# Sparse attention of one block in a single written order: products between the groups of heads, the index sum on TensorE

## The chip, the cores and the metric

The kernel runs on one core of a Trainium2 chip. A core has five engines that run side by side, each with its own list of instructions: TensorE (PE, matrix products), VectorE (DVE), ScalarE (ACT), GpSimd (POOL) and SyncE (SP, which here only starts transfers). They wait for one another by semaphores. The metric is the device time of one execution in microseconds (us). The profile adds the clock that TensorE was granted, as a share of its full 2.4 GHz; the lower of its two levels, 1.2 GHz, reads 0.50.

## The reference

The model is two blocks on 256 tokens of width 1024, with a batch of one. Only one part of the first block is touched by the change, the sparse attention (16 heads of 64 for the queries; one key and one value head; 8 index heads):

```python
def sparse_attention(h, cos, sin, w_in, q_norm, k_norm, w_out, topk):
    q, k, v, qi, ki, wi = split_cols(h @ w_in, SA_SPLITS)
    q = apply_rope(rms_norm(q...), cos, sin); k = ...; qi, ki = apply_rope(...)
    # for each block of 128 queries:
    logits = einsum('bthd,bsd->btsh', qi, ki)
    score = einsum('btsh,bth->bts', relu(logits), wi) * idx_scale
    score = where(causal, score, -inf)
    _, sel = top_k(score, topk)                  # 64 keys of each row
    s = einsum('bthd,btkd->bthk', q, k[sel]) * att_scale
    p = softmax(where(valid, s, -inf))
    o = einsum('bthk,btkd->bthd', p, v[sel])
    return o @ w_out
```

The kernel does not gather. It finds the 64 largest scores of a row, and adds 0 to the logits of the chosen keys and a very negative number to all others.

## The kernel before, in words

**Products.** Every weight matrix is kept in float32 and split into two float32r parts, hi (a copy by ACT, line 201) and lo (the difference, line 205, in pieces of 512 columns; where `help` is set, POOL takes the second piece). A product is then three matmuls, hi by hi, hi by lo and lo by hi (`mm3`, lines 276, 277 and 278), most of them 512 columns wide. `fetch` loads 128x2048 of weights (three such buffers), `halve` makes hi and lo of one half (four of each).

**Sparse attention.** Tokens come as two tiles t of 128. The steps have a letter each. P: the products of key, value, index key and index weights (200 columns). K: their rope (norm and rotation). J: the transposes to kT. R and T: rope and transposes of the index queries of a tile. L: the index logits, a matmul of 64 partitions for each of 8 heads, and relu into `rl`. S: the index sum (lines 978 to 991): on DVE, eight operations a tile that add relu times the weight of the head to a running sum, then the causal limit. C: the choice of the 64 largest, two rounds of 8 in each of four parts (lines 1002 and 1003), and the bias. U and M: load of and product with the query weights of a group g of 8 heads. Q and X: scale and rope of a group and tile. Y: its transposes.

**Attention proper** goes through 12 items (t, g, b): the scores of four heads (tile 0, 128 keys) or two heads (tile 1, 256 keys), 512 columns each. A (`attend`, line 1059): matmuls into one PSUM bank, then on DVE the sum with the bias and the maximum of every head (1062, 1064). Z (`exps`, 1072): exponentials on ACT. B (`probs`, 1081, 1083): four transposes on PE and a copy by ACT. O (`values`, 1092): products with the values. F (`finish`): division by the sums, and four transposes (`flip`, line 433) with a split, which make the stationary operand of the output product. In the loop, round i issues A of item i, Z of item i-1, B of i-2 and O of i-3.

**What sets the order.** Inside this part every engine takes its instructions in the order in which the program writes them. `ORDER` gives all steps up to the first item, then, between bars, what goes in after the A of each round. W loads a unit of the output weights, and D is one step of `down_steps`, the output product (8 k-tiles, two halves of 512 columns, two token tiles). The last two D begin after the last bar of items; the final part of `down_steps` issues the last k-tiles together with the entry of the next part. `mid` there does the transposes of the fourth finished group (line 433, at 923.42 us in the profiled execution); from that point on both kernels do the same work.

Of the kernel before, what the change touches and what calls it, by code (L numbers as in the profile page):

```python
# [18 lines left out]
T = 256  # L19
# [9 lines left out]
class Wide:  # L29
    """Transposed activations, split in two float32r parts: k-tiles of [128 features, 256 tokens]."""  # L30
# [72 lines left out]
class Net:  # L103
# [52 lines left out]
    def consts(self):  # L156
# [40 lines left out]

# [9 lines left out]
    def rsqrt(self, v, n, scale=1.0, add=EPS):  # L207
        """1 / sqrt(v * scale + add), [128, n]; add may be a column."""
# [9 lines left out]
    def row_rstd(self, x):  # L218
        """[128, 1] of 1/sqrt(mean(x*x) + eps), x [128, 1024]."""
# [6 lines left out]
    def softplus(self, y, n):  # L226
        """max(y, 0) + log1p(exp(-|y|)); log1p(u) = 2 atanh(u / (2 + u)) as a series (|argument| <= 1/3)."""
# [31 lines left out]
    def halve(self, raw, h, help=False):  # L259
        """Half h of the columns as (hi, lo)."""  # L260
# [7 lines left out]
    def unit(self, dram, cols=2048, help=(0, 0)):  # L268
        """Load [128, cols], give two (hi, lo) halves."""
# [3 lines left out]
    def mm3(self, out, a, b, start, stop):  # L273
        """out += a^T b with a = (hi, lo), b = (hi, lo)."""
# [15 lines left out]
    def group_steps(self, dram, hT):  # L290
        """group_x in two steps, a yield in between."""
# [14 lines left out]
    def weave(self, main, side, done):  # L306
        """Emit main, with as many steps of side as it gives in between; done gets an item when main is through."""
# [25 lines left out]
    def down_steps(self, dram, n, aT, done, then, ready={}, mid=lambda: None):  # L333
# [4 lines left out]
        acc = [[self.ps() for _ in range(2)] for _ in range(2)]  # L338
        def go(t, cb, kk, w):
            s = slice(cb * 512, cb * 512 + 512)  # L340
            self.mm3(acc[t][cb], aT(kk, t), (w[0][:, s], w[1][:, s]), kk == 0, kk == n - 1)
        late = []
        for u in range(n // 2):
            for h, w in enumerate(ready.get(u) or self.unit(dram[u])):
# [7 lines left out]
            yield  # L352
        a, b, *cd = late
# [4 lines left out]
        def last(t, cb):  # L358
            for k in cd:
                go(t, cb, *k)  # L360
            done(t, cb, acc[t][cb])
# [8 lines left out]
        with self.manual():  # L370
            whole(0, a)
            whole(0, b)
            mid()
# [50 lines left out]
    def to_T(self, t, src, aT, gain=None):  # L424
        """src [128 tokens, 1024] -> k-tiles of aT for token tile t (times gain[:, k])."""
# [3 lines left out]
    def flip(self, src, aT, b, t, gain=None):  # L429
        """src [128 tokens, 512] -> half b of aT, token tile t."""  # L430
# [5 lines left out]
    def put_T(self, p, aT, b, t, gain):  # L436
        """Transposed [128, 4, 128] in PSUM (times gain) -> half b of aT, token tile t."""
# [4 lines left out]
        # the two engines take turns at a PSUM bank: each all of it at a time  # L442
# [37 lines left out]
    def start(self, dram):  # L480
        """The first part's start: loads in the order of their use; the clock of TensorE is up by then."""
# [57 lines left out]
class Hybrid:  # L539
    def hybrid(self, then):  # L540
# [8 lines left out]
        def products():  # L549
            """The wide products that only wait for the input: z, q, k, v and the output gate."""  # L550
# [30 lines left out]
        def chain():  # L581
            """Gives how many steps of the wide products may go in here."""
# [38 lines left out]
            bc = self.g().rearrange("p (j t c) -> p j t c", j=4, t=2)     # B0 B1 C0 C1  # L621
# [10 lines left out]
            def inputs(g):  # L632
                """x of one group of 8 heads, token-major, before its activation"""
# [9 lines left out]
            def states(g):  # L643
# [4 lines left out]
                # state after the first chunk: B^T (x dt decay)  # L648
# [7 lines left out]
            def decays(g):  # L656
                """per chunk of 128 tokens: scores times decays [s, head, t]"""
# [44 lines left out]
            # scores C B^T (transposed), B of the first chunk token-major  # L702
# [32 lines left out]
            R = self.t2()                   # R0 R1 wi wk rows  # L735
# [13 lines left out]
            w = self.small(16)              # exp(-m_t) (2 chunks), w_inter, state weights  # L749
# [25 lines left out]
            # state of the first chunk  # L775
# [67 lines left out]
ORDER = ("P0 P1 R0 U00 K U01 R1 M000 T0 J M001 L0 T1 S0 U10 C00 M010 M011 L1 X00 C01 S1 M100 C02 X01 Q00 C03 M101 "  # L843
         "Y00 C10 U11 C11 Q01 Y01 C12 | C13 M110 | M111 X10 |  | Y10 X11 |  | Q10 Q11 Y11 |  |  |  |  |  | "
         "W0 | D | W1 | D | ")
SHARE = ((0, 0), (0, 0), (1, 1), (1, 1), (1, 1), (1, 1))

TURN = (0, 0, 0, 1, 0, 1)


class Sparse:
    def rope_setup(self):
        """cos and sin of position * frequency, [128, 2, 32] each."""
# [14 lines left out]
        self.cs = self.const(128)           # cos (2 x 32), sin (2 x 32)  # L868
# [4 lines left out]
        # tables (c, s) times the gain of q; times that of k, and plain for the index key  # L873
# [15 lines left out]
    def rope(self, out, x, c, s, H, copies=1, help=0):  # L889
        """out[:, h, copy, :] = x rotated; c, s [128, H or 1, 2, 32] broadcast; x [128, H, 64]."""  # L890
        V = self.nc.vector
        W = self.nc.gpsimd if help else V
# [9 lines left out]
        W.tensor_tensor(o5[:, :, :, 0], both(a4[:, :, 0]), both(b4[:, :, 1]), OP.subtract)  # L902
        W.tensor_tensor(o5[:, :, :, 1], both(a4[:, :, 1]), both(b4[:, :, 0]), OP.add)

    def sparse(self, then):
# [6 lines left out]
        plain = lambda f, t: cs[:, f, t][:, None, None].to_broadcast([128, 8, 2, 32])  # L912
        gained = lambda f, t: self.cq4(f)[:, t].rearrange("p (h d) -> p h d", h=2)[:, None].to_broadcast([128, 8, 2, 32])

# [5 lines left out]
        kk = self.t2().rearrange("p (h r d) -> p h r d", h=4, r=2)    # (t, i), twice  # L920

        def keys(u):
            for h, w in enumerate(self.unit(ins["saw"][:, u * 800:(u + 1) * 800], 800)):
                hi, lo = (a.rearrange("p (k c) -> p k c", k=2) for a in w)
                for k in range(2):
                    i = 4 * u + 2 * h + k
                    for t in range(2):
                        self.mm3(pk[t][:, :200], hT.tok(i, t), (hi[:, k, :], lo[:, k, :]), i == 0, i == 7)

        def key_rope():  # L930
            ss = self.small(2)
            for t in range(2):
                A.activation(kv[:, t, :200], pk[t][:, :200], AF.Copy)
                A.activation(self.junk[:, :64], pk[t][:, :64], AF.Square, accum_out=ss[:, t:t + 1])
            r = self.rsqrt(ss, 2, 1.0 / 64)
            c, s = (self.ck[:, f * 256:f * 256 + 256].rearrange("p (h f d) -> p h f d", h=4, f=2) for f in range(2))
            self.rope(kk, kv.rearrange("p t (i d) -> p (t i) d", i=2)[:, :, :64], c, s, 4, 2)
# [847 lines left out]
```

## Time and profile before

| | |
|---|---|
| time, median of 3 runs | 1735.54 us (1732.81 to 1738.21) |
| the profiled execution: its span | 1757.1 us, 23,334 instructions |
| TensorE busy | 1720.3 us, 98% of the span |
| VectorE, ScalarE, GpSimd busy | 63%, 51%, 18% |
| loaded from memory | 283 MB, 163 GB/s over the span |
| the touched part | about 811 to 923 us of the span |

The profiled execution took its span of 1757.1 us with the profiler on, 1.2% more than the median of the runs; times inside it are read against its own span. A "busy" PE is a PE with a matmul in flight, at whichever clock: the share of 98% does not tell how fast it went. Durations of matmuls overlap, so that the cost of one in a sequence is the distance from start to start.

### The profile page before, as it was taken

What the parts mean: (1) busy time and instruction counts of PE and PEld (TensorE: products, weight loads), DVE (VectorE), ACT (ScalarE), POOL (GpSimd) and SP (SyncE); (2) the same over time, 40 slices, a digit from 0 to 9 for tenths busy, and PEclk for the clock granted to TensorE, in tenths of its full rate; (3) what the DMA queues carried; (4) which work ended last, traced back from release to release, by engine and by line L of the source; (5) the groups of instructions that cost most, each with busy time, mean ns of one, the idle gap of its engine ahead of it and who ended that gap; (6) DMA issues with size and microseconds to landing.
All of it is one profiled execution on the core that took longest, in us unless ns stands there. A gap on an engine that the chain in (4) does not pass through costs nothing.

```text
span 1757.1 us, 23334 instructions
## 1 busy us (share of the span) xinstructions
PE 1720.3 (98%) x8742; PEld 1437.8 (82%) x8742; DVE 1111.6 (63%) x2107; ACT 902.7 (51%) x1323; POOL 318.1 (18%) x466
## 2 busy tenths in 40 slices
PE   9999999999999999999899999999999999999998
PEld 7888799887888888887688888788898878879886
DVE  6555588666555565547736564557775765678565
ACT  6544476465444454435445544466446446745643
POOL 3000121001000100002311000233632124264211
PEclk9999999999999999999669999999999999999999
DMA  7545453445455554554114555455544444544442
GB/s 269 189 173 199 146 192 121 144 158 185 173 191 191 180 184 176 193 188 151 40 66 174 192 174 216 140 174 168 156 145 150 158 155 168 168 134 167 156 144 96
DMA packets 63425, 287.40 MB, mean 164 GB/s; under 512 B 23760, under 2 KB 26704, under 8 KB 30288
## 3 DMA queue, kind: packets, MB, share of 16 engines
q1 hardware_dynamic: 63312, 285.92, 46.5%
q8 instruction: 68, 1.11, 0.3%
q14 instruction: 45, 0.37, 0.1%
HBM read 283.28 MB, written 2.62 MB: 163 GB/s over the span
## 4 chain that ended last, share of the span: by engine, by line
PE 81%; POOL 6%; DVE 4%; issue 4%; DMA 2%; ACT 2%; SPq 1%; POOLq 0%; ACTq 0%; DVEq 0%
PE mm L277 24%; PE mm L278 24%; PE mm L276 24%; POOL g L1320 2%; POOL g L1318 2%; PE tr L433 1%; PE tr L468 1%; DMA g<-dram 1%; ACT hi L201 1%; DVE lo L205 1%; POOL lo L205 1%; DMA dram<-g 1%; DVE g L85 1%; POOL sm L215 0%; DVE g L987 0%
## 5 line engine op out<-in xcount | busy, mean ns | idle before, releaser
L205 DVE TENSOR_TENSOR lo<-raw,hi 128x512 fp32r<-128x512 f32 (+1 forms) x1024 | 694.8, 720 | 406.1 <-ACT hi L201 404.6
L201 ACT ACTIVATE hi<-raw 128x1024 fp32r<-128x1024 f32 x530 | 551.5, 1045 | 455.3 <-PE mm L278 317.7
L277 PE MATMUL mm<-lo,g 128*128 128x512 f32 (+1 forms) x1440 | 576.9, 401 | 0.8 <-DVE lo L205 0.5
L276 PE MATMUL mm<-hi,g 128*128 128x512 f32 (+1 forms) x1440 | 576.5, 403 | 0.7 <-ACT g L201 0.7
L278 PE MATMUL mm<-hi,g 128*128 128x512 f32 (+1 forms) x1440 | 571.5, 397 | 0.3 <-DVE g L446 0.2
L278 PEld LDWEIGHTS mm<-hi,g 128*128 128x128 f32 x1440 | 273.8, 190 | 62.8 <-DVE g L205 1.6
L277 PEld LDWEIGHTS mm<-lo,g 128*128 128x128 f32 x1440 | 274.0, 190 | 61.5 <-DVE lo L205 3.9
L276 PEld LDWEIGHTS mm<-hi,g 128*128 128x128 f32 x1440 | 273.9, 190 | 60.2 <-ACT g L201 1.2
L277 PE MATMUL mm<-lo,f 128*128 128x512 f32 x416 | 165.2, 397 | 0.2 <-POOL lo L205 0.2
L278 PE MATMUL mm<-hi,f 128*128 128x512 f32 x416 | 164.8, 397 | 0.0
L276 PE MATMUL mm<-hi,f 128*128 128x512 f32 x416 | 163.6, 400 | 0.0
L276 PE MATMUL mm<-g,hi 128*128 128x256 f32 x480 | 136.3, 284 | 0.0
L278 PE MATMUL mm<-g,lo 128*128 128x256 f32 x480 | 135.8, 285 | 0.0
L277 PE MATMUL mm<-g,hi 128*128 128x256 f32 x480 | 135.2, 282 | 0.0
L212 POOL TENSOR_SCALAR sm<-sm 128x1 f32<-128x1 f32 x18 | 9.4, 521 | 562.2 <-ACT c L70 561.1
L277 PEld LDWEIGHTS mm<-lo,f 128*128 128x128 f32 x416 | 78.4, 188 | 19.0 <-POOL lo L205 0.6
L278 PEld LDWEIGHTS mm<-hi,f 128*128 128x128 f32 x416 | 78.3, 188 | 18.5
L276 PEld LDWEIGHTS mm<-hi,f 128*128 128x128 f32 x416 | 78.5, 189 | 18.2
L276 PEld LDWEIGHTS mm<-g,hi 128*128 128x128 f32 x480 | 90.6, 189 | 0.7 <-issue 0.2
L277 PEld LDWEIGHTS mm<-g,hi 128*128 128x128 f32 x480 | 90.5, 189 | 0.3
L278 PEld LDWEIGHTS mm<-g,lo 128*128 128x128 f32 x480 | 90.1, 188 | 0.4 <-issue 0.2
L201 ACT ACTIVATE g<-tr 128x512 fp32r<-128x512 f32 x48 | 28.1, 595 | 86.9 <-PE tr L433 57.1
(387 smaller groups left out, 1693.9 us busy)
## 6 DMA issues: line engine op xcount, KB each, us to landing
raw<-in_wgu_dram SPq DMA_DIRECT2D x86, 1024.0 KB, 4.8
raw<-in_wdn_dram SPq DMA_DIRECT2D x44, 1024.0 KB, 4.8
raw<-in_bx_dram SPq DMA_DIRECT2D x24, 1024.0 KB, 4.9
raw<-in_bgate_dram SPq DMA_DIRECT2D x24, 1024.0 KB, 4.9
raw<-in_bw_dram SPq DMA_DIRECT2D x20, 1024.0 KB, 5.0
raw<-in_hyx_dram SPq DMA_DIRECT2D x12, 1024.0 KB, 4.8
raw<-in_bproj_dram SPq DMA_DIRECT2D x12, 1024.0 KB, 5.0
raw<-in_hyw_dram SPq DMA_DIRECT2D x10, 1024.0 KB, 4.8
```

The costliest lines, as they stand in the source:

```text
L85: self.nc.vector.scalar_tensor_tensor(self.src[t][:, s], self.net.x[t][:, s], self.rstd[t], self.gain[:, s], op0=OP.mult, op1=OP.mult)
L201: nc.scalar.activation(hi, src, AF.Copy)
L205: (nc.gpsimd if o and help else nc.vector).tensor_tensor(lo[..., s], src[..., s], hi[..., s].bitcast(F32), OP.subtract)
L212: G.tensor_scalar(r, v, add, EPS, op0=OP.add, op1=OP.add)
L276: mm(out, a[0], b[0], start=start, stop=False)
L277: mm(out, a[0], b[1], start=False, stop=False)
L278: mm(out, a[1], b[0], start=False, stop=stop)
L433: self.nc.tensor.transpose(p[:, k, :], src[:, k * 128:(k + 1) * 128], self.ident)
L468: nc.tensor.transpose(p[:, t, j, :], hd[:, j * 128:(j + 1) * 128], self.ident)
L1318: G.tensor_tensor(a, Z[:, :m, e:e + 1].to_broadcast([128, m, n]), B[:, e:e + 1, cs].to_broadcast([128, m, n]), OP.mult)
L1320: G.tensor_tensor(Z[:, :m, cs], Z[:, :m, cs], a, OP.add)
```

## The change

The part gets one written order for all its steps, the rounds of items included, and smaller steps: query loads by half a unit (U), query products by k-tile (M for both token tiles of group 0, N for one of group 1), output loads by half (W), and output products by token tile, k-tile and column half (D). A product of one k-tile and one token tile is three matmuls; group 1 has sixteen. In before, eight of these precede the first item and eight follow the A of items 0 and 1, and all output products but those left to a later step follow the A of the last item. Now fourteen of the sixteen and 20 output products stand between the steps of the items. The keys are loaded in one fetch of 1600 columns with two halves of 800 in place of four of 400; the rope of the key is done apart from that of the index key. No piece of lo and no rope is on POOL any more.

The index sum becomes matmuls: ACT scales the identity by the weight of each head (`index_weights`, 16 copies of 128x128), and eight float32 matmuls a tile add diagonal times relu in a PSUM bank (`index_scores`). ACT copies the first half of tile 1; DVE keeps the causal limit.

```diff
-ORDER = ("P0 P1 R0 U00 K U01 R1 M000 T0 J M001 L0 T1 S0 U10 C00 M010 M011 L1 X00 C01 S1 M100 C02 X01 Q00 C03 M101 "
-         "Y00 C10 U11 C11 Q01 Y01 C12 | C13 M110 | M111 X10 |  | Y10 X11 |  | Q10 Q11 Y11 |  |  |  |  |  | "
-         "W0 | D | W1 | D | ")
-SHARE = ((0, 0), (0, 0), (1, 1), (1, 1), (1, 1), (1, 1))
-TURN = (0, 0, 0, 1, 0, 1)
+ORDER = (
+    "H0 R0 H1 P0 P1 U000 R1 U001 E U010 T0 M00 K1 G0 J1 U011 T1 L0 M01 S0 K0 M02 L1 U100 G1 C00 J0 M03 C01 S1 U101 "
+    "M04 C02 M05 U110 C03 M06 C10 M07 Q00 U111 X00 Q01 C11 N00 X01 N01 Y00 C12 "
+    "A0 N02 Z0 N03 Y01 C13 N04 "
+    "A1 N05 B0 Z1 N06 N07 O0 Q10 "
+    "A2 N10 B1 Z2 N11 N12 O1 X10 F0 "
...
+    "A7 D021 B6 Z7 I1 D031 O6 "
...
+    "A11 D041 W30 B10 Z11 D050 O10 "
+    "W31 B11 D051 O11 F3")
...
+        def index_weights(t):
+            dg[t] = self.g(1024).rearrange("p (h s) -> p h s", h=8)
+            for h in range(8):
+                A.activation(dg[t][:, h, :], self.ident, AF.Copy, scale=wi[:, t, h:h + 1])
...
         def index_scores(t):
             S = 128 * (t + 1)
-            z = sc[t] = self.g(256)
+            z = sc[t] = self.l2(256)
+            pz = self.pt()[:, :S]
             for jb in range(2):
                 for r in range(2):
                     for i in range(2):
-                        h = 4 * jb + 2 * i + r
-                        x = rl[t, jb, r][:, i, :S]
-                        if jb + r + i:
-                            V.scalar_tensor_tensor(z[:, :S], x, wi[:, t, h:h + 1], z[:, :S], op0=OP.mult, op1=OP.add)
-                        else:
-                            V.tensor_scalar(z[:, :S], x, wi[:, t, h:h + 1], None, op0=OP.mult)
-            tr = z[:, S - 128:S]
-            V.tensor_tensor(tr, tr, self.causal, OP.min)
+                        mm(pz, dg[t][:, 4 * jb + 2 * i + r, :], rl[t, jb, r][:, i, :S], start=jb + r + i == 0,
+                           stop=jb + r + i == 3)
+            if t:
+                A.activation(z[:, :128], pz[:, :128], AF.Copy)
+            V.tensor_tensor(z[:, S - 128:S], pz[:, S - 128:], self.causal, OP.min)
...
-            w[g, u] = self.unit(ins["sax"][2 + 2 * g + u], help=SHARE[2 * g + u])
+            if h == 0:
+                w[g, u] = self.fetch(ins["sax"][2 + 2 * g + u])
+            w[g, u, h] = self.halve(w[g, u], h)
...
+        def down(t, kk, cb):
+            go(t, cb, kk, w["o", kk])
...
-            first, *then_ = ORDER.split("|")
-            do(first)
-            late = []
-            for i, names in enumerate(then_):
...
+            for o in ORDER.split():
+                args = (int(o[1:]),) if o[0] in "AZBO" else map(int, o[1:])
+                steps[o[0]](*args)
+        self.down_end(go, acc, [(k, w["o", k]) for k in range(4, 8)], self.add_x, then, lambda: turned(3))
```

On PE, in the middle of the items, before (1059 is A, 1081 B, 1092 O, 433 the transposes of a finished group):

```order
L1092 MATMUL tr_7299<-l_985_6824,t_1131_7426 128x64 x4
L1059 MATMUL mm_7460<-l_987_6826,g_7333 128x128 x4
L1081 MATMUL tr_7475<-c_71,t_1118_7379 128x128 x4
L1092 MATMUL tr_7299<-l_985_6824,t_1139_7454 128x64 x4
L1059 MATMUL mm_7490<-l_987_6826,g_7410 128x256 x2
L1081 MATMUL tr_7501<-c_71,t_1137_7437 128x128 x4
```

And after, on PE between the A of items 6 and 7 (1100 is A, 1123 B, 1135 O, 1078 Y; 276 to 278 are an output product):

```order
L1100 MATMUL mm_7502<-l_987_6826,g_7430 128x128 x4
L276 MATMUL mm_7463<-hi_7467,f_6829 128x512
L277 MATMUL mm_7463<-lo_7468,f_6829 128x512
L278 MATMUL mm_7463<-hi_7467,f_6830 128x512
L1123 MATMUL tr_7516<-c_71,t_1135_7457 128x128 x4
L1078 MATMUL tr_7527<-c_71,t_1140_7481 128x128 x4
L276 MATMUL mm_7534<-hi_7370,f_6829 128x512
L277 MATMUL mm_7534<-lo_7371,f_6829 128x512
L278 MATMUL mm_7534<-hi_7370,f_6830 128x512
...
L1135 MATMUL tr_7314<-l_985_6824,t_1150_7521 128x64 x4
L1100 MATMUL mm_7548<-l_987_6826,g_7430 128x128 x4
```

The narrow matmuls of an item are the same; three output products of three matmuls each have come between two A (one is left out here).

On DVE, the index sum of tile 1, before (989, 987 and 991 are the sum, 1002 and 1003 the choice for tile 0):

```order
L1003 MATCH_REPLACE l_1034_7044<-sm_7105,l_1034_7044 128x128
L989 TENSOR_SCALAR g_7108<-t_1038_7078,sm_6825 128x256
L987 SCALAR_TENSOR_TENSOR g_7108<-t_1038_7078,sm_6825,g_7108 128x256
L987 SCALAR_TENSOR_TENSOR g_7108<-t_1040_7083,sm_6825,g_7108 128x256 x2
L987 SCALAR_TENSOR_TENSOR g_7108<-t_1042_7088,sm_6825,g_7108 128x256 x2
L987 SCALAR_TENSOR_TENSOR g_7108<-t_1044_7093,sm_6825,g_7108 128x256 x2
L991 TENSOR_TENSOR g_7108<-g_7108,c_82 128x128
L1002 MAX sm_7132<-l_1034_7044 128x8
```

And after, on DVE from the end of the first half of U01 to the first choice of tile 0 (1028 is the causal limit of tile 0, which now reads a PSUM bank; 921 to 974 are the rope of the key):

```order
L205 TENSOR_TENSOR lo_6967<-raw_6925,hi_6966 128x512 x2
L1028 TENSOR_TENSOR l_1027_7004<-tr_7005,c_82 128x128
L921 TENSOR_TENSOR t_1030_7020<-l_985_6824,c_286 128x128
L922 TENSOR_TENSOR t_1031_7021<-l_985_6824,c_286 128x128
L923 TENSOR_TENSOR t_988_6827<-t_1030_7020,t_1031_7021 128x2x2x32
L924 TENSOR_TENSOR t_988_6827<-t_1030_7020,t_1031_7021 128x2x2x32
L974 TENSOR_TENSOR t_988_6827<-t_988_6827,sm_7017 128x2x128
L205 TENSOR_TENSOR lo_7056<-raw_7053,hi_7055 128x512 x2
L1039 MAX sm_7070<-l_1027_7004 128x8
```

Of the sum only the limit is left on DVE; the splits and the rope of the key stand behind it.

## Rows read from the trace of the kernel before

**Rows 1.** The page: the span, and the granted clock in 40 slices.
```profile
span 1757.1 us, 23334 instructions
...
PEclk9999999999999999999669999999999999999999
```

**Rows 2.** Windows: us, busy (count) of PE, PEld, DVE, ACT, POOL, PEclk, DMA, GB/s.
```profile
811.00:838.00 27.00, 27.00 (x166) 22.64 (x165) 24.34 (x57) 12.92 (x25) 3.57 (x4) 1.00 0.54 194
838.00:845.00 7.00, 1.82 (x10) 1.18 (x8) 6.55 (x22) 3.08 (x4) 2.43 (x4) 0.72 0.00 0
845.00:862.00 17.00, 14.73 (x59) 10.91 (x60) 16.24 (x57) 6.71 (x20) 6.50 (x9) 0.80 0.26 93
862.00:904.40 42.40, 42.40 (x163) 36.01 (x162) 16.50 (x68) 22.41 (x63) 8.49 (x12) 0.50 0.00 1
904.40:923.40 19.00, 18.81 (x94) 15.26 (x94) 8.74 (x12) 8.26 (x13) 3.49 (x2) 0.96 0.45 166
```

**Rows 3.** Groups on DVE, 811 to 862 us: count, busy us, mean ns, idle before.
```profile
L205 DVE TENSOR_TENSOR lo<-raw,hi 128x512 fp32r<-128x512 f32 x12 | 9.5, 849 | 0.0
L987 DVE SCALAR_TENSOR_TENSOR g<-t,sm,g 128x128 f32<-128x128 f32 x7 | 4.3, 620 | 0.5
...
L987 DVE SCALAR_TENSOR_TENSOR g<-t,sm,g 128x256 f32<-128x256 f32 x7 | 3.4, 485 | 0.5
...
L902 DVE TENSOR_TENSOR t<-t,t 128x256 f32<-128x256 f32 x5 | 2.1, 424 | 0.2
```

**Rows 4.** Timeline of DVE: start us, us, line, operation.
```profile
846.57 3.26 DVE L205 TENSOR_TENSOR lo<-raw,hi 128x512 fp32r<-128x512 f32 x2
...
854.02 0.28 DVE L1062 CUSTOM_DVE_ANT_0 t<-mm,l 128x128 f32<-128x128 f32 x1
```

**Rows 5.** ACT: the relus of tile 1; durations of scaled copies 128x128 (min/median/max).
```profile
831.50 2.07 ACT L976 ACTIVATE t<-tr 128x512 f32<-128x512 f32 x4 [4.12 <-PE tr L973]
...
L444 ACT ACTIVATE g<-tr,c x32: 349/368/408, 4.8 to 1669.0; 128x128 fp32r<-128x128 f32 x32
```

**Rows 6.** Timeline of PE, index logits of tile 1 to the first items.
```profile
830.33 2.10 PE L973 MATMUL tr<-l,g 64*128 64x256 f32 x16
...
843.85 1.11 PE L1039 MATMUL tr<-c,t 128*128 128x128 f32 x4 [5.18 <-POOL t L903]
...
853.45 0.50 PE L276 MATMUL mm<-hi,g 128*128 128x512 f32 x1
853.78 0.39 PE L277 MATMUL mm<-lo,g 128*128 128x512 f32 x1
...
856.42 1.13 PE L1059 MATMUL mm<-l,g 64*128 64x256 f32 x4
857.48 0.66 PE L1081 MATMUL tr<-c,t 128*128 128x128 f32 x4
```

**Rows 7.** Timeline of PE among the items: A of two rounds.
```profile
864.01 2.07 PE L1059 MATMUL mm<-l,g 64*128 64x256 f32 x4
...
868.66 2.07 PE L1059 MATMUL mm<-l,g 64*128 64x256 f32 x4
```

**Rows 8.** Timeline of PE, output products and the last steps of items.
```profile
906.13 0.40 PE L277 MATMUL mm<-lo,f 128*128 128x512 f32 x1
...
910.80 0.60 PE L1081 MATMUL tr<-c,t 128*128 128x128 f32 x4
911.23 1.00 PE L1092 MATMUL tr<-l,t 128*128 128x64 f32 x8
912.07 0.61 PE L1081 MATMUL tr<-c,t 128*128 128x128 f32 x4
...
923.42 0.60 PE L433 MATMUL tr<-c,t 128*128 128x128 f32 x4
```

**Rows 9.** Windows again: the clock's rise after the items; a stretch of another part.
```profile
904.40:905.90 1.50, 1.50 (x6) 1.21 (x6) 0.00 (x0) 1.26 (x5) 0.00 (x0) 0.50 0.97 235
...
1672.40:1679.20 6.80, 6.80 (x48) 6.25 (x47) 2.62 (x7) 2.94 (x3) 0.00 (x0) 1.00 0.11 48
```

More of the change, by code (lines that the diff above doesn't have):

```diff
@@ L331, in down, with down_go, down_steps @@
             pass
-    def down_steps(self, dram, n, aT, done, then, ready={}, mid=lambda: None):
-        acc = [[self.ps() for _ in range(2)] for _ in range(2)]
+    def down_go(self, n, aT):
+        acc = {}
         def go(t, cb, kk, w):
             s = slice(cb * 512, cb * 512 + 512)
-            self.mm3(acc[t][cb], aT(kk, t), (w[0][:, s], w[1][:, s]), kk == 0, kk == n - 1)
+            if (t, cb) not in acc:
+                acc[t, cb] = self.ps()
+            self.mm3(acc[t, cb], aT(kk, t), (w[0][:, s], w[1][:, s]), kk == 0, kk == n - 1)
+        return go, acc
+    def down_steps(self, dram, n, aT, done, then):
+        go, acc = self.down_go(n, aT)
         late = []
         for u in range(n // 2):
-            for h, w in enumerate(ready.get(u) or self.unit(dram[u])):
+            for h, w in enumerate(self.unit(dram[u])):
                 kk = 2 * u + h
@@ L352, in down_steps, with down_end @@
             yield
+        self.down_end(go, acc, late, done, then)
+    def down_end(self, go, acc, late, done, then, mid=None):
         a, b, *cd = late
@@ L370, in down_steps @@
         with self.manual():
-            whole(0, a)
-            whole(0, b)
-            mid()
+            if mid:
+                mid()
+            else:
+                whole(0, a)
+                whole(0, b)
             if E.norm:
@@ L887, in ck5, with rope @@
         return self.ck[:, f * 256:f * 256 + 256].rearrange("p (t i d) -> p t i d", t=2, i=2)[:, :, i]
-    def rope(self, out, x, c, s, H, copies=1, help=0):
+    def rope(self, out, x, c, s, H, copies=1):
         V = self.nc.vector
-        W = self.nc.gpsimd if help else V
         n = H * 64
@@ L901, in rope @@
         V.tensor_tensor(b4, x4, s, OP.mult)
[L902 to L903 removed]
+        V.tensor_tensor(o5[:, :, :, 0], both(a4[:, :, 0]), both(b4[:, :, 1]), OP.subtract)
+        V.tensor_tensor(o5[:, :, :, 1], both(a4[:, :, 1]), both(b4[:, :, 0]), OP.add)
     def sparse(self, then):
@@ L919, in sparse @@
         v = kv[:, :, 64:128]
-        kk = self.t2().rearrange("p (h r d) -> p h r d", h=4, r=2)
-        def keys(u):
[L923 to L928, printed above, removed]
@@ L930, in key_rope @@
-        def key_rope():
-            ss = self.small(2)
-            for t in range(2):
[L933 to L937, printed above, removed]
-            k = kk.rearrange("p (t i) r d -> p t i (r d)", t=2)[:, :, 0]
-            V.tensor_tensor(k, k, r[:, :, None].to_broadcast([128, 2, 128]), OP.mult)
-            V.tensor_scalar(wi, kv[:, :, 192:200], 8.0 ** -0.5 * 64.0 ** -0.5, None, op0=OP.mult)
@@ L942, in key_flip, with key_load @@
-        def key_flip():
-            pT = self.pt().rearrange("p (i t s) -> p i t s", i=2, t=2)
-            for t in range(2):
-                for i in range(2):
-                    PE.transpose(pT[:, i, t], kk[:, 2 * t + i].rearrange("p r d -> p (r d)"), self.ident)
-            A.activation(kT, pT, AF.Copy)
+        kk = self.t2().rearrange("p (t i r d) -> p t i r d", t=2, i=2, r=2)
+        key_ss = self.small(2)
+        w = {}
+        def key_load(u):
+            if u == 0:
+                w["k"] = self.fetch(ins["saw"], 1600)
+            w["k", u] = self.halve(w["k"], u)
@@ new lines, in keys, with key_out @@
+        def keys(u):
+            hi, lo = (a.rearrange("p (k c) -> p k c", k=4) for a in w["k", u])
+            for k in range(4):
+                i = 4 * u + k
+                for t in range(2):
+                    self.mm3(pk[t][:, :200], hT.tok(i, t), (hi[:, k, :], lo[:, k, :]), i == 0, i == 7)
+        def key_out():
+            for t in range(2):
+                A.activation(kv[:, t, :192], pk[t][:, :192], AF.Copy)
+            for t in range(2):
+                A.activation(wi[:, t], pk[t][:, 192:200], AF.Copy, scale=8.0 ** -0.5 * 64.0 ** -0.5)
@@ new lines, in key_rope @@
+        def key_rope(i):
+            if i == 0:
+                for t in range(2):
+                    A.activation(self.junk[:, :64], kv[:, t, :64], AF.Square, accum_out=key_ss[:, t:t + 1])
+                r = self.rsqrt(key_ss, 2, 1.0 / 64)
+            c, s = (self.ck5(f, i) for f in range(2))
+            k = kk[:, :, i]
+            self.rope(k, kv[:, :, 128 * i:128 * i + 64], c4(c), c4(s), 2, 2)
+            if i == 0:
+                k = k.rearrange("p t r d -> p t (r d)")
+                V.tensor_tensor(k, k, r[:, :, None].to_broadcast([128, 2, 128]), OP.mult)
@@ L950, in sparse, with key_flip @@
+        def key_flip(i):
+            pT = self.pt()[:, :256].rearrange("p (t s) -> p t s", t=2)
+            for t in range(2):
+                PE.transpose(pT[:, t], kk[:, t, i].rearrange("p r d -> p (r d)"), self.ident)
+            A.activation(kT[:, i], pT, AF.Copy)
         pq = {}
-        half = lambda S: kT[:, 1].rearrange("p t s -> p (t s)")[:, :S]
         v8 = lambda a: a.rearrange("p (h d) -> p h d", h=8)
-        w, qi, qTi, rl, sc, bias, qTs, sc_q, state, P = ({} for _ in range(10))
+        qi, qTi, rl, sc, bias, qTs, sc_q, state, P, dg = ({} for _ in range(10))
@@ L1006, in choose, with load, product, both @@
                 V.tensor_scalar(wk, wk, -BIG, None, op0=OP.mult)
[L1009 to L1019 removed]
+        def load(g, u, h):
+            if h == 0:
+                w[g, u] = self.fetch(ins["sax"][2 + 2 * g + u])
+            w[g, u, h] = self.halve(w[g, u], h)
+        def product(g, kk, t):
+            if (g, t) not in pq:
+                pq[g, t] = self.ps()
+            self.mm_x(pq[g, t], hT, kk, t, w[g, kk // 4, kk // 2 % 2])
+        def both(kk):
+            for t in range(2):
+                product(0, kk, t)
         def scale(g, t):
             sq = self.t2()
[L1023 removed]
+            A.activation(sq, pq[g, t], AF.Square)
             ss = self.small(8)
@@ L1044, in sparse, with attend @@
         cat = Wide(self.f, 2)
-        def attend(t, g, b):
+        items = [(t, g, b) for g in range(2) for t in range(2) for b in range(2 * (t + 1))]
+        def attend(n):
+            t, g, b = items[n]
             S = 128 * (t + 1)
@@ L1100, in finish @@
                             OP.mult)
-            return lambda: self.flip(o, cat, g, t)
-        units = {}
-        out = self.down_steps(ins["sao"], 8, cat.tok, self.add_x, then, units, lambda: late.pop()())
-        def prepare(u):
-            units[u] = self.unit(ins["sao"][u], help=SHARE[4 + u])
-        steps = {"P": keys, "K": key_rope, "J": key_flip, "R": index_rope, "T": index_flip, "L": index_logits, "S": index_scores, "C": choose, "U": load,
-                 "M": product, "X": turn, "Q": scale, "Y": flip, "D": lambda: next(out), "W": prepare}
@@ L1111, in sparse @@
-        items = [(t, g, b) for g in range(2) for t in range(2) for b in range(2 * (t + 1))]
-        def do(names):
-            for o in names.split():
-                steps[o[0]](*map(int, o[1:]))
-        with self.manual():
-            first, *then_ = ORDER.split("|")
-            do(first)
-            late = []
-            for i, names in enumerate(then_):
-                for lag, step in enumerate((attend, exps, probs, values)):
-                    if 0 <= i - lag < len(items):
-                        step(*items[i - lag])
-                    if lag == 0:
-                        do(names)
-                        while late and i - 3 < len(items):
-                            late.pop()()
-                if 0 <= i - 3 < len(items) and items[i - 3][2] == 2 * items[i - 3][0] + 1:
-                    late.append(finish(*items[i - 3][:2]))
@@ L1131, in sparse, with turned, prepare @@
-        for _ in out:
-            pass
+        def turned(n):
+            self.flip(done[n], cat, *divmod(n, 2))
+        go, acc = self.down_go(8, cat.tok)
+        def prepare(u, h):
+            if h == 0:
+                w["r", u] = self.fetch(ins["sao"][u])
+            w["o", 2 * u + h] = self.halve(w["r", u], h)
+        def down(t, kk, cb):
+            go(t, cb, kk, w["o", kk])
+        steps = {"H": key_load, "P": keys, "E": key_out, "K": key_rope, "J": key_flip, "R": index_rope, "T": index_flip,
+                 "G": index_weights, "L": index_logits, "S": index_scores, "C": choose, "U": load, "M": lambda _, kk: both(kk),
+                 "N": lambda t, kk: product(1, kk, t), "X": turn, "Q": scale, "Y": flip, "A": attend, "Z": exps,
+                 "B": probs, "O": values, "F": finish, "I": turned, "W": prepare, "D": down}
```

47 lines of the change are left out of this document (21 added, 26 removed), and 7 rows, old and new, of the table ORDER.

## The prediction, made before the changed kernel had run

> **What bounds the kernel now.** I read the page first. Its clock row shows one dip, to six tenths in two of forty slices, close to the middle of the span; everywhere else TensorE has nearly its full clock [rows 1]. A PE that is busy 98% of the span gains nothing from shorter waits in general, but this place runs slow. The windows by stage, read next, put the dip into the sparse attention: 811 to 838 us at 1.00, 838 to 845 at 0.72 with PE busy 1.82 of 7.00, 845 to 862 at 0.80, 862 to 904.40 at 0.50 with PE busy all the time, and 904.40 to 923.40 at 0.96 [rows 2]. Two limits follow. From 838 to about 857 DVE bounds: it is busy 6.55 of 7.00 and 16.24 of 17.00 while PE waits, once 5.18 us in one piece for a rope [rows 2, 6]. From 862 to 904.40 PE bounds, at 1.2 GHz: a round of one item takes 4.65 us from A to A (864.01 to 868.66) [rows 7]. The timelines then give pieces at either clock; they are the prices below.
>
> The part ends, for my purpose, at 923.42, the transposes of the last finished group [rows 8]: behind that both kernels have the same work. So the question is when those transposes come.
>
> **Up to the first item: DVE.** The reduction of the first A runs on DVE at 854.02 [rows 4]. What moves it:
> - Index sum taken from DVE: seven operations a tile, 4.3 and 3.4 us, with 0.5 idle before each group, gives 8.7 less [rows 3].
> - POOL's pieces of lo: two DVE pieces took 3.26 us at 846.57 [rows 4]; the other ten of the twelve took 9.5 - 3.26 = 6.2, or 0.62 each [rows 3]. The two would take 1.2, so 2.0 less if POOL working on the same buffers is what slows them. But four pieces come over from POOL, 4 x 0.62 = 2.5 more, and half a rope, 2 x 0.42 = 0.8 more [rows 3]. The rope of the key in two pieces costs some 0.4 more, one operation of the same kind.
> - Keys loaded in two halves rather than four quarters: DVE is idle 27.00 - 24.34 = 2.7 us from 811 to 838 [rows 2], nearly all of it there; I take 2.7 less.
> - New waits of DVE. ACT makes each hi in the order written, and DVE is strict in its order too. Lo of U01's first half stands behind four copies of the key outputs on ACT, which wait for the last key product: 2.0. The limit of S0 waits for eight matmuls and eight copies on ACT; behind it on DVE stand the key's rope, a split and the choice: 2.8. Lo of U10 waits for a hi behind relus, 2.07 for four [rows 5], with a start: 2.9. The limit of S1 waits likewise: 1.8. Together 9.5; these are estimates from my own chain of durations.
>
> The sum: -8.7 - 2.0 - 2.7 + 2.5 + 0.8 + 0.4 + 9.5 = -0.2. I take no gain: the first reduction stays at 854.0, and the first B at 857.5 as now [rows 4, 6], 3.5 us later. If all four waits lie beside other work it is 9.7 less, and if they are half as long again, 5 more.
>
> The 16 new copies cost ACT at most 16 x 0.37 = 5.9 us [rows 5]; ACT is busy 12.92 of 27.00 there [rows 2], so they hide, apart from S0's wait. The diagonal matmuls add PE work: 3072 columns of float32. Lower bound: the logits, 2.10 us for 2048 columns with two halves of the array in turn [rows 6], so 3.2. Upper: A, 1.06 us for 512 columns (856.42 to 857.48) [rows 6], so 6.4. I take 6.4, since all go into one bank and take all partitions, as no logits do. Either way PE, idle 5.2 us of 838 to 845 [rows 2], absorbs it behind DVE; without that cover the end moves by 3 to 6. The Trainium skill, "FP8 and Floating Point Precision", section "TensorE Precision Notes", says true float32 takes four passes of the array. By that, 3072 x 4 / 2.4 GHz = 5.1 us is an estimate between the two; the sum doesn't change.
>
> **From the first B to the end: PE.** At 857.5 there are left in the new order, at full clock:
> - A of items 2 to 11: 10 x 1.06 = 10.6 [rows 6].
> - B of 12 items, 0.43 each (910.80 to 911.23), 5.2; O of 12, 0.84 each (911.23 to 912.07), 10.1 [rows 8].
> - 30 products: 10 of group 1 and 20 of the output. Twenty matmuls lie between 906.13 and 910.80, 0.2335 each [rows 8], so 0.70 a product: 21.0. A first one after narrow work takes 0.33 (853.45 to 853.78) [rows 6], 0.1 more; 23 such groups give 2.3.
> - Five sets of transposes (two Y, three of finished groups) at 0.43: 2.2.
> - The tail: B of the last item waits for its exponentials, F for its last values; I allow 0.5 and 1.3.
>
> Sum 10.6 + 5.2 + 10.1 + 21.0 + 2.3 + 2.2 + 1.8 = 53.2; 857.5 + 53.2 = 910.7. Add a clock that must rise first: PE still waits for DVE ahead of the first item, as it does now, where 845 to 862 went at 0.80, a loss of 3.4 us of full clock [rows 2]. I charge 2.0 and get 912.7, which is 10.7 earlier than 923.42.
>
> Where does the gain come from? The same narrow work costs 42.4 us now at half clock; at full clock it would be 21.2 less. Half of that is spent again: ten products of group 1 (7.0) that PE now does before the first B, beside DVE's chain, come behind it, the starts of 23 short groups cost 2.3, and 2.0 is charged for a clock that has to rise.
>
> Does the mix keep the clock? In the present trace 904.40 to 905.90 still reads 0.50 [rows 9], while all of 904.40 to 923.40 reads 0.96 [rows 2], so the rest of it went at 1.00: the rise came 1.5 us after wide products began. Elsewhere 6.80 us with 48 matmuls ran at 1.00 [rows 9]; wide ones of 0.2335 would fill that with 29, so most were narrow. In the new order about 21 of 53 us are wide products, in runs of one to three.
>
> ACT and DVE keep pace: a round of the mix takes PE about 53 / 11 = 4.8 us, while a B starts 857.48 - 854.02 = 3.5 after its reduction [rows 4, 6]; in the new order 4 to 5 us of PE work lie between. DVE, busy 16.50 of 42.40 now [rows 2], gets about 12 splits of weights more, at 2 x 0.62: 15 us, and about a rope a round; it fits in 53.
>
> **Scale.** The span of 1757.1 against a median of 1735.54 gives 0.988. 10.7 x 0.988 = 10.6, so 1735.5 - 10.6 = 1724.9, say 1725.
>
> **The rivals.**
> - Gain of the index sum kept: the waits I charged are hidden, and the first reduction comes 8 us earlier, near 846. For it: 8.7 us of DVE work really goes, and DVE bounds there. Against it: two engines are now in the chain that DVE alone was. 1725 - 8 = 1717. Chance 0.2.
> - Items wait on one another: if exponentials and copies come late by 0.7 us in each of 12 rounds, 8.4 us go. For it: ACT now has relus, splits, flips and exponentials in one strict line. Against it: ACT was busy 22.41 of 42.40 [rows 2]. 1725 + 8 = 1733. Chance 0.15.
> - The other side: the clock stays at 1.2 GHz in the mix. All PE work from the first B on then takes up to 2 x 53 = 106 us, and the end comes at about 961, 38 later than now; the time is near 1772. It decides from where half clock covers more than about 21 us of the stretch (10.7 us of gain lost, at half a us for every us). For it: the clock stays low through 42.4 us of a PE that is busy all the time [rows 2]; so busy alone does not raise it, and runs of three products may not. At 847 to 851, too, products ran slow for a while after the wait, in the window at 0.80 [rows 2]. Against it: the quick rise, and the 48 mostly narrow matmuls at 1.00 [rows 9]. The Trainium skill, "TensorE: Matmul & The Clock Gate", section "PE-mode transpose", says transposes don't count as busy to the clock gate as other matmuls do; B and Y are of that kind, 7 of 53 us here. That is too little to decide it, and no run here shows the rule apart. Chance 0.12, with cases in which only part of the stretch is slow, 1741 to 1772.
> - The change does not do what it says: a buffer or a PSUM bank makes PE take the steps as late as now, and the products only change places. The rounds are then as long as their latencies and the time stays at 1735. Against it: products of items and output have banks of their own now. Chance 0.05.
>
> **How the numbers follow.** The forecast has a chance of 0.48, and its own range is 1719 to 1731. Below lies the first rival, down to 1711 with a clock that never dips; above the second, to 1738. The range 1711 to 1738 leaves out most of the slow clock and little else. This kernel's times tell 0.3%, 5.2 us, from none. Faster than 1730.3: nearly the whole of the forecast (0.45) and the first rival (0.2), 0.65. Slower than 1740.7: the slow clock (0.12) and the worst of the second and last rivals (0.05), 0.17. The same: 0.18.
>
> **What would show it.** In the profile after, the windows from the first B on should read a clock near 1.00 and PE busy throughout, with three narrow pieces and one to three products between two A in 4.5 to 5 us. The first reduction on DVE should lie about 43 us behind 811 in before's count; earlier by 5 or more means that the first rival is right. A slow clock shows at once, as an A of 2.0 us. I am wrong in the main step if the clock reads 0.50 there, or if PE has idle time in every round with ACT as the releaser.

## The result

The changed kernel takes 1750.0 us (median of 4 runs, 1749.33 to 1752.2), the kernel before 1736.9 (4 runs, 1732.81 to 1739.07). The ratio is 1.0082, with an interval of 1.0069 to 1.0094: 0.8% slower. 1725 was forecast, and faster.

The profile after, the page's span and clock:

```profile
span 1750.4 us, 23371 instructions
...
PEclk9999999999999999999899999999999999999999
```

Its span, 1750.4 us, is 6.7 us shorter than that of before [rows 1], and the dip of the clock has almost gone. So the profiled executions say faster, and the runs say slower. Both hold, as the experiments show: the profiled execution of before was not like most of its runs.

The same stretches as in [rows 2], of after (us; busy time and count of PE, PEld, DVE, ACT, POOL; granted clock; DMA share; GB/s):

```profile
811.00:838.00 27.00, 24.12 (x157) 20.01 (x156) 15.93 (x38) 16.80 (x43) 0.90 (x2) 1.00 0.34 118
838.00:845.00 7.00, 7.00 (x32) 5.75 (x31) 5.59 (x19) 2.76 (x4) 0.00 (x0) 1.00 0.24 70
845.00:862.00 17.00, 10.42 (x41) 7.94 (x40) 16.21 (x54) 4.46 (x9) 5.54 (x8) 0.70 0.26 94
862.00:904.40 42.40, 42.03 (x244) 34.25 (x244) 24.12 (x88) 28.09 (x77) 4.74 (x8) 1.00 0.18 63
904.40:923.40 19.00, 17.88 (x96) 14.11 (x96) 9.57 (x24) 8.71 (x17) 2.59 (x2) 1.00 0.31 111
```

The mix runs at 1.00 with PE busy 42.03 of 42.40. DVE is no longer nearly full from 811 to 838 (15.93 of 27.00); it waits there now, and is full from 845 to 862, where PE waits. DVE's waits of after, 811 to 862 us (in total, times, longest):

```profile
DVE lo L205 <- ACT hi L201: 9.0, 5, 3.8
DVE l L1028 <- PE tr L1024: 3.3, 1, 3.3
DVE l L1028 <- ACT l L1027: 0.5, 1, 0.5
```

What DVE no longer adds up, it waits for: 12.8 us, most of it for hi parts that stand in ACT's line behind copies and relus. Rows of the timelines of after, on PE and (1103) on DVE; 814.18 is the first key product, 1024 the sum by diagonals, with the start of what follows it on PE, 1078 Y, 1123 B, 1100 A, 445 the transposes of a group:

```profile
814.18 0.26 PE L276 MATMUL mm<-hi,g 128*128 128x200 f32 x1
...
827.92 1.95 PE L1024 MATMUL tr<-t,g 128*128 128x128 f32 x16
829.63 0.48 PE L276 MATMUL mm<-hi,g 128*128 128x512 f32 x1
...
835.72 3.87 PE L1024 MATMUL tr<-t,g 128*128 128x256 f32 x16 [0.65 <-ACT g L1002]
839.24 0.58 PE L276 MATMUL mm<-hi,g 128*128 128x512 f32 x1
...
852.48 1.09 PE L1078 MATMUL tr<-c,t 128*128 128x128 f32 x4 [5.89 <-DVE t L924]
...
858.52 0.28 DVE L1103 CUSTOM_DVE_ANT_0 t<-mm,l 128x128 f32<-128x128 f32 x1
...
862.67 0.82 PE L1123 MATMUL tr<-c,t 128*128 128x128 f32 x4
...
870.27 1.13 PE L1100 MATMUL mm<-l,g 64*128 64x256 f32 x4
...
875.32 1.13 PE L1100 MATMUL mm<-l,g 64*128 64x256 f32 x4
...
916.69 0.66 PE L445 MATMUL tr<-c,t 128*128 128x128 f32 x4 [0.78 <-DVE t L1145]
```

Against [rows 4, 6 to 8]: an item now takes 5.05 us with three products in it (870.27 to 875.32), where it took 4.65 with none at half clock; PE's wait ahead of the items is still there, 5.89 for 5.18.

A table of the part, from the first key product on, makes kernels comparable whose profiled executions lose a few us elsewhere. Each number is the start in the timeline less that of the first key product; "end" is the transposes of the last group (923.42 in before, 916.69 in after). The lower eight rows belong to the experiments.

| kernel | first reduction | first B | A of item 4 | end | clock in the items |
|---|---|---|---|---|---|
| before (profiled) | 42.9 | 46.4 | 52.9 | 112.3 | 0.50 |
| after | 44.3 | 48.5 | 61.1 | 102.5 | 1.00 |
| warm_before | 43.0 | 47.7 | 52.5 | 92.5 | 1.00 |
| order_only | 45.8 | 49.6 | 62.6 | 104.0 | 1.00 |
| early_g1 | 44.3 | 48.1 | 63.0 | 108.7 | 0.72 |
| warm_after | 44.3 | 47.5 | 62.7 | 104.1 | 0.96 |
| warm_early_g1 | 44.3 | 50.9 | 62.6 | 102.6 | 1.00 |
| fewer_products | 44.3 | 48.4 | 58.7 | 99.6 | 1.00 |
| sum_t1 | 40.4 | 43.6 | 50.9 | 95.0 | 0.90 |
| warm_sum_t1 | 40.4 | 44.0 | 49.7 | 89.7 | 1.00 |

### The profile page after: what moved, and what is told of

Its sections match the earlier page's. It is cut to its first block, busy times and chain, and to the rows that moved or that the text cites. A ratio compares the mean times of both kernels' runs of the same rounds, so it can differ in the third digit from the quotient of the medians.

```text
span 1750.4 us, 23371 instructions
## 1 busy us (share of the span) xinstructions
PE 1710.0 (98%) x8774; PEld 1425.0 (81%) x8774; DVE 1106.6 (63%) x2106; ACT 907.6 (52%) x1341; POOL 306.8 (18%) x454
## 4 chain that ended last, share of the span: by engine, by line
PE 83%; POOL 6%; DVE 4%; DMA 3%; ACT 2%; issue 2%; SPq 0%; POOLq 0%; ACTq 0%; DVEq 0%
PE mm L277 24%; PE mm L276 24%; PE mm L278 24%; POOL g L1358 2%; POOL g L1356 2%; DVE lo L205 1%; PE tr L445 1%; DMA g<-dram 1%; PE tr L480 1%; ACT hi L201 1%; POOL lo L205 1%; DMA raw<-in_wgu_dram 1%; DMA dram<-g 1%; DVE g L85 1%; PE tr L1135 0%
## 5 line engine op out<-in xcount | busy, mean ns | idle before, releaser
L205 DVE TENSOR_TENSOR lo<-raw,hi 128x512 fp32r<-128x512 f32 x1032 | 696.4, 717 | 406.0 <-ACT hi L201 404.3
```

The source lines that it names most:

```text
L205: (nc.gpsimd if o and help else nc.vector).tensor_tensor(lo[..., s], src[..., s], hi[..., s].bitcast(F32), OP.subtract)
```

## The experiments

Each was timed beside before on the same chip: before_again, order_only, sum_only and early_g1 on one, the other six on another.

**before_again** is the kernel before, with no edit.

> The kernel before, unchanged. Theory A (the profiled execution of before was not like its timed runs: TensorE ran at 1.2 GHz through the items in the profile only, and 42.4 us at half clock are 21 us too many, which is the 1757.1 of its span against 1735.5): the new profile has a span of about 1735, a granted clock of 0.98 to 0.99, a clock near 1.00 in most of the stretch of the items, and the transposes of the last group lie about 91 us behind the first key product, not 112. Rival B (the low clock belongs to the kernel, and the profiled execution lost its 21 us elsewhere): the items are at 0.50 again, 40 us and more, and the span is the shorter by other stretches.

Of 12 executions ten took 1734.6 to 1739.6 us, at a mean granted clock of 0.989 to 0.993, and two 1756.5 and 1759.5, at 0.978 and 0.976. Of 35 more runs of before, timed beside it, four took 1756.2 to 1759.2. The profiled one was again one of the two, with its mean clock and its window of the items (columns as above):

```profile
core 0: 1757.7 us, clock 0.976
```

```profile
862.00:904.40 42.40, 42.40 (x163) 35.99 (x162) 16.78 (x69) 22.45 (x62) 8.49 (x12) 0.50 0.00 1
```

The ten usual runs of the same kernel have spans of 1732.5 to 1736.8, so 20.9 to 25.2 us less; 42.4 us at half clock are 21.2 too many. Their mean clocks agree: at the lowest, 0.989 over 1736.8 us, all the time at half clock in the whole execution adds up to 2 x 0.011 x 1736.8 = 38 us, less than 42.4, so in none of the ten can the items have run at 0.50 throughout. That is theory A, but the trace again shows only the long kind. The next kernel shows the other.

**warm_before** adds matmuls that nobody reads where PE waits.

```diff
+        def fill(*n):
+            p = self.pt()
+            for _ in range(int("".join(map(str, n)))):
+                mm(p, hT.tok(0, 0)[0], hT.half[0][0][:, 0].rearrange("p k c -> p (k c)"), start=True, stop=True)
...
-         "Y00 C10 U11 C11 Q01 Y01 C12 | C13 M110 | M111 X10 |  | Y10 X11 |  | ..."
+         "Y00 V20 C10 U11 C11 Q01 Y01 C12 | C13 M110 | M111 X10 |  | V5 Y10 X11 |  | ..."
```

> The kernel before with matmuls that nobody reads (20 of 512 columns while PE waits for the rope of the second tile, 5 ahead of the transposes in round 3). If a PE that waits is what lowers the clock, and the items then run at whichever level they find: all runs near 1733 to 1736, none near 1757, the items at a clock of 1.00 in the profile, and the transposes of the last group 88 to 92 us behind the first key product. If the slower runs of before have another cause: some runs near 1757 still, or a clock of 0.50 in the items.

12 runs of 1730.6 to 1738.0, median 1735.2, clock 0.993 to 0.997, none long; ratio 0.9983 (0.9961 to 1.0004). The windows, and then the timeline of PE (812.04 is the first key product, 859.78 the first B; 1059 is A, 1081 B, 1092 O, 433 the transposes of a group):

```profile
838.00:845.00 7.00, 6.37 (x32) 4.93 (x31) 6.48 (x21) 3.10 (x4) 1.55 (x3) 1.00 0.00 0
845.00:862.00 17.00, 14.82 (x59) 10.74 (x59) 16.27 (x55) 5.95 (x19) 7.39 (x10) 0.80 0.26 93
862.00:904.40 42.40, 42.20 (x264) 35.30 (x263) 27.54 (x85) 30.55 (x75) 12.57 (x14) 1.00 0.21 75
```

```profile
812.04 0.26 PE L276 MATMUL mm<-hi,g 128*128 128x200 f32 x1
...
859.78 0.66 PE L1081 MATMUL tr<-c,t 128*128 128x128 f32 x4
...
864.49 1.13 PE L1059 MATMUL mm<-l,g 64*128 64x256 f32 x4
865.55 0.65 PE L1081 MATMUL tr<-c,t 128*128 128x128 f32 x4
866.04 1.00 PE L1092 MATMUL tr<-l,t 128*128 128x64 f32 x8
866.98 1.13 PE L1059 MATMUL mm<-l,g 64*128 64x256 f32 x4
...
904.56 0.60 PE L433 MATMUL tr<-c,t 128*128 128x128 f32 x4
```

The same instructions as in [rows 7] take 2.49 us an item (864.49 to 866.98) in place of 4.65, and the part ends 92.5 us after the first key product, not 112.3. So these narrow items can run at either level. The usual time stayed as it was, so this trace is taken to stand for a usual run of before. That the 25 extra matmuls removed the long kind is not shown: before had only one long run in 26 (1755.3) beside these twelve.

**order_only**: the new order, with the index sum on DVE (`index_scores` of before, G0 and G1 out of the order).

> The new order with the index sum on DVE as in before. If the diagonal form of the sum is what costs (two engines in DVE's chain): faster than the changed kernel, 1740 to 1745. If the order costs (ten products of group 1 and 23 short groups put behind the first B, about 9 us, and a later first item): the sum's 8.7 us come back onto DVE, less the waits of DVE at the limit of S0 (3.3 us) and of S1, so 3 to 6 us slower than the changed kernel, 1753 to 1756.

1748.9 (1745.9 to 1751.4), ratio 1.0049 (1.0022 to 1.0077): neither figure. The ratio counts the four long runs of before; by medians it is 1748.9 against 1737.3. The order alone makes nearly the whole loss, 11.5 us of 13.1, as the second theory said, but the sum's form is worth next to nothing in it: DVE's sum puts the first reduction 1.4 us later than after's, and the runs are 1 us shorter.

**sum_only**: the old order with both sums as products with a diagonal.

```diff
-"... T0 J M001 L0 T1 S0 U10 C00 M010 M011 L1 ..."
+"... T0 J M001 G0 L0 T1 S0 U10 C00 G1 M010 M011 L1 ..."
```

> The old order with the index sum as products with a diagonal (16 scaled copies on ACT, 16 matmuls). If the order alone makes the change slow: faster than before by the 8.7 us taken from DVE less its new waits of about 4.6, so 1730 to 1734. If the diagonal form costs: slower than before, 1740 and above, with DVE idle at the two causal limits for more than 8 us.

A miss. Four of 12 runs took 1740.7 to 1744.1 (clock near 0.99), eight 1754.7 to 1757.8 (0.98). The first reduction came 41.0 us after the first key product, 1.9 sooner, and yet no run was below 1740; the long kind, six of 47 in before on that chip, became the common one. The profiled execution was of that kind, so this case cannot say where the others lost 4 us.

**early_g1**: all products of group 1 ahead of the first B.

```diff
-    "... X00 Q01 C11 N00 X01 N01 Y00 C12 " "A0 N02 Z0 N03 Y01 C13 N04 " "A1 N05 B0 Z1 N06 N07 O0 Q10 " ...
+    "... X00 Q01 C11 N00 N01 N02 N03 N10 N11 N12 N13 X01 Y00 C12 " "A0 N04 N05 N14 N15 Z0 Y01 C13 "
+    "A1 N06 N07 N16 N17 B0 Z1 O0 X10 Q10 X11 Q11 " "A2 B1 Z2 O1 F0 " "A3 W00 B2 Z3 I0 O2 " ...
```

> The changed kernel with all sixteen products of group 1 before the first B, as in before (eight before the first A, eight behind A of items 0 and 1), and the ropes of group 1 behind O0; the output products stay between the items. If the moved products are what the change lost: 7.0 us and some starts leave the stretch behind the first B and fill PE's wait ahead of the first item, 1741 to 1744. If the rounds of items are bound by their latencies, or if the first item comes later by as much: 1748 to 1752.

1756.0 (1751.7 to 1757.7), above both figures, and slower than the change itself. PE now waits inside the rounds, and the clock falls there (the O of item 1 in the timeline of PE, then windows with busy PE, clock, DMA, GB/s):

```profile
866.07 1.97 PE L1135 MATMUL tr<-l,t 128*128 128x64 f32 x8 [2.31 <-ACT t L1125]
```

```profile
862.00:864.00 2.00, 1.76 (x8) 0.72 0.03 8
864.00:866.00 2.00, 0.00 (x0) 0.50 0.00 0
...
884.00:886.00 2.00, 2.00 (x8) 0.50 0.49 168
886.00:888.00 2.00, 2.00 (x13) 0.80 0.97 403
```

From 864 to 886 it stays at 0.50. The products had been covering a latency of the items, here the wait of O for ACT's copy behind B: in the new order B of an item stands ahead of the A after next, and PE, in the order written, stands with it.

**warm_after**: the changed kernel with 22 unread matmuls ahead of Y00 (`N00 X01 N01 V22 Y00`).

> The changed kernel with 22 such matmuls ahead of the first transposes of queries, where PE waits 5.9 us. If the low clock from 850 to 861 is worth what it takes from PE there: 2 to 4 us faster than the changed kernel, 1746 to 1748; the rest of the difference to before stays. If DVE alone sets the first item: 1750, the same.

1751.5 (1748.9 to 1753.7): the second figure, the same as the change. The window 845 to 862 went to 1.00, the first reduction stayed at 44.3, and 862 to 880 read 0.91 instead. So the clock's dip ahead of the items does not set the first reduction. What the dip costs by itself this run does not tell, as a low clock came back behind it and the part ended at 104.1, later than after's 102.5.

**warm_early_g1**: early_g1 with unread matmuls in two rounds (`B0 Z1 V3 O0`, `A2 V6 B1 Z2 V6 O1`).

> All sixteen products of group 1 ahead of the first B (as in early_g1), with 3, 6 and 6 such matmuls in the rounds of items 1 and 2, where PE waited for ACT and the clock fell. If the low clock from 863 to 886 is why early_g1 was slow: 10 to 12 us faster than it, 1744 to 1746, and faster than the changed kernel. If the rounds without products are bound by the latency of an item: 1752 or more even at full clock.

1747.1 (1743.1 to 1752.9), 9 us below early_g1, so the low clock was most of what it lost. But the part ends at 102.6, as in after, with no query product behind the first B. This does not price the waits of the items, as the unread matmuls stand in the products' place (1165, in the timeline of PE):

```profile
861.54 0.95 PE L1165 MATMUL tr<-g 128*128 128x512 f32 x3
...
864.57 1.64 PE L1165 MATMUL tr<-g 128*128 128x512 f32 x6
...
866.40 1.64 PE L1165 MATMUL tr<-g 128*128 128x512 f32 x6
```

From their start to the next one's on PE they take 4.0 us, the first B is 2.4 us later than in after, and the waits of O for ACT's copy are 1.2 us in all.

**fewer_products**: the changed kernel without N06 and N11 to N16.

> The changed kernel with seven of the ten query products of group 1 behind the first B left out (k-tile 6 of token tile 0, k-tiles 1 to 6 of tile 1), so part of the queries is not computed. If PE is the bound from the first B on, so that each product moved there costs its full time: 7 x 0.70 and three short groups' starts, 5.2 us faster than the changed kernel, 1744 to 1746. If the rounds are held by exponentials and copies: under 2 us faster, 1748 or more.

1748.1 (1746.9 to 1755.0). The part ends 2.9 us sooner than after's (99.6 for 102.5), where 5.2 and under 2 were expected: a little over half of the time of the products is given back. The windows from the first B to the end, of after and of this kernel (columns as in the first windows):

```profile
862.67:916.69 54.02, 52.53 (x303) 42.30 (x301) 30.32 (x102) 33.99 (x86) 4.74 (x8) 1.00 0.20 70
```

```profile
858.79:909.99 51.20, 48.58 (x282) 38.23 (x280) 30.17 (x102) 34.21 (x86) 4.74 (x8) 1.00 0.22 74
```

PE is busy for 3.9 us less, and idle for 1.1 more.

**sum_t1**: before with the diagonal form for tile 1 alone, whose limit can stand late.

```diff
-"... S0 U10 C00 M010 M011 L1 X00 C01 S1 M100 C02 X01 Q00 C03 M101 Y00 C10 ..."
+"... S0 U10 C00 G1 M010 M011 L1 X00 C01 M100 I1 C02 X01 Q00 C03 M101 Y00 S1 C10 ..."
```

Here I is the eight matmuls and ACT's copy, S1 only the limit.

> The kernel before with the diagonal form for tile 1 alone, whose sum is needed late (eight products of the queries lie between the relus and the sum's matmuls, the causal limit stands behind the rope). DVE loses 4.2 us of sums and gains no wait. If DVE's chain sets the first item of before also at full clock: 3 to 4 us faster than before, 1732 to 1734 in most runs. If PE is the bound there, or the new 3.9 us of PE work come into the way: 1737 or more.

1737.6 (1732.8 to 1743.8), no gain. The first reduction came 2.6 us sooner than in warm_before (40.4 for 43.0), so DVE's chain does set it; the clock took it back (windows of PE):

```profile
854.00:856.00 2.00, 1.23 (x4) 1.00 0.00 0
856.00:858.00 2.00, 1.47 (x5) 0.67 0.00 0
858.00:860.00 2.00, 1.88 (x10) 0.50 0.00 0
...
868.00:870.00 2.00, 2.00 (x9) 0.50 0.00 0
870.00:872.00 2.00, 2.00 (x17) 0.92 0.00 0
```

**warm_sum_t1** puts 17 unread matmuls where that PE waited (`C13 V5 M110 | M111 X10 | V6 | V6 Y10 X11`).

> The kernel before with the diagonal form for tile 1 alone and 17 matmuls that nobody reads (5 ahead of the second half of the third load's products, 6 in each of rounds 2 and 3), where PE waited and the clock fell in the profile of sum_t1. If what sum_t1 gained on DVE (the first reduction 2.6 us sooner after the first key product) was lost to the clock of 856 to 871 us: 1731 to 1733, faster than before in every run. If PE is behind by its own work whatever DVE does: 1735 to 1737, as warm_before.

1732.8 (1730.9 to 1736.2, 12 runs), ratio 0.9984 (0.9975 to 0.9992): 0.16% faster than before, and the best of all kernels here. The window of the items' start, 0.80 in before and 0.70 in after, reads full (columns as in the first windows):

```profile
845.00:862.00 17.00, 16.67 (x86) 12.49 (x85) 15.31 (x59) 9.15 (x29) 4.53 (x7) 1.00 0.26 93
862.00:904.40 42.40, 42.22 (x254) 35.15 (x254) 26.30 (x74) 27.33 (x66) 12.76 (x15) 1.00 0.28 100
```

One run, at 1736.2, was above before's median of 1735.8; "faster in every run" was too much.

## Why the prediction was wrong

**The step that failed** is the scale: "The span of 1757.1 against a median of 1735.54 gives 0.988", and with it the start of the whole sum, a stretch from 862 to 904.40 at 0.50. I spread the 21.6 us between profile and runs evenly over the span. They sat in the one stretch that I wanted to make faster: half of 42.4 is 21.2. In the usual run of before this stretch is not at half clock, as the mean clocks of before_again show; at full clock, in warm_before, the end comes after 92.5 us in place of 112.3. The gain that I forecast was one over a kind of execution that two of 12 are.

**Inside that execution the sum was right.** From the first key product the end came 112.3 - 102.5 = 9.8 us sooner, for 10.7 forecast. Term by term:
- First reduction: no change forecast, 1.4 later measured. DVE's new waits were put at 9.5; the trace has 12.8, of which S0's limit 3.3 for 2.8. (The 8.7 counts seven of the eight operations of a tile's sum.)
- Diagonal matmuls: 6.4 taken, 1.71 + 3.52 = 5.2 measured from start to start (827.92 to 829.63, 835.72 to 839.24), inside the bounds of 3.2 and 6.4. The Trainium skill's four passes ("FP8 and Floating Point Precision", section "TensorE Precision Notes") gave an estimate of 5.1; the trace agrees, and it decided nothing.
- First B to the end: 53.2 + 2.0 forecast, 916.69 - 862.67 = 54.0 measured.
- The clock kept 1.00 through the mix; the rival of a slow clock did not happen. The time came out inside its 1741 to 1772 by chance, for another reason.

**Against the usual before the same terms make a loss.** The forecast end is 912.7 - 811.08 = 101.6 us behind the first key product. Set against warm_before's 92.5, the same sum says 9.1 us slower; measured is an end at 102.5, 10.0 slower. Of these 0.8 are there at the first B, and 9.2 come between it and the end, which take 54.0 us in after and 44.8 in warm_before:

```profile
859.78:904.56 44.78, 44.59 (x275) 37.01 (x274) 29.73 (x90) 32.59 (x83) 12.57 (x14) 1.00 0.20 71
```

PE is busy for 44.59 us of that, and for 52.53 of 54.02 in after, so it is PE's own work that sets this stretch, and the work has grown: by ten products of group 1 and the starts of short groups, which the forecast priced at 7.0 and 2.3 and counted as "spent again". Waits add 1.3, and warm_before has five unread matmuls there that after lacks, 1.3: 7.0 + 2.3 + 1.3 - 1.3 = 9.3. The products used to lie beside DVE's chain; PE's wait there did not shrink in return (5.89 us for 5.18). The A of item 4 in the table, 8.6 later, does not split this loss by place, because by then the new order has done one B and two O that the old one does later.

Taking the products away brings back less than they cost. Without seven of the ten, 4.9 us by the forecast's price, the part ends 2.9 sooner (fewer_products). With none of them behind the first B, O waits for ACT's copy, 3.3 us in all in early_g1, and there the clock falls too. The old order has B two rounds behind A and O three; the new one has both B and O one round behind. That the shorter lag causes these waits is argued from the order, not tried by itself.

**The index sum** costs or gives about 1 us in the new order (order_only); my 8.7 us from DVE came back as waits of DVE, as I had charged.

**Open.** The runs differ by 13.1 us, the part by 10.0. The remaining 3 must lie in other stretches, where the clock dips at differing places from one execution to the next. Whether the change has a hand in that, no run here tells: over the twelve traces the first key product starts at 810.2 to 814.2 us, and what follows the end of the part takes 829.3 to 835.8, with both orders spread over both ranges. Nor is it known what decides, in an execution of before, whether the clock falls at about 862 us, or whether unread matmuls prevent it.

## What to carry to other kernels

Compare the profiled execution's span with the runs before any sum: where they differ by a per cent, look for a stretch whose clock accounts for the difference, and forecast for the kind of execution that the median is. Work that lies beside another engine's chain is free only there; moved behind it, into a stretch that PE fills, it costs PE's time. Matmuls put between steps hide latency, but the old order, with more rounds of lag, had next to no waits without them (PE busy 44.59 of 44.78 us in warm_before).

## What was not expected of the hardware

The same narrow matmuls ran for 42 us at 0.50 with PE busy throughout in two profiled executions of before. In its usual executions, with nothing changed in the program, the mean clock of 0.989 to 0.993 leaves no room for that, and in warm_before they ran at 1.00. In sum_t1 the clock rose at about 870 us among them, without a wide product. Seventeen matmuls that nobody reads, put where PE waited in sum_t1, took the clock of its items from 0.90 to 1.00 in the profiles and the median from 1737.6 to 1732.8 us (warm_sum_t1).
